# Two edits in a two-layer diffusion backbone: the low parts of the last tokens' normed activations from GpSimd to VectorE, and the first projection's matmuls between halves of the modulation's

## The chip, the cores and the metric

The kernel runs on one core of a Trainium2 chip. A core has TensorE (matrix multiplies into PSUM banks), VectorE, ScalarE and GpSimd (elementwise work), SyncE (here it only issues DMAs), an on-chip memory of 128 partitions (SBUF), and DMA queues to HBM. Each engine takes its own instructions strictly in order; engines wait for each other through semaphores. In the profile the engines are called PE (with PEld for its weight loads), DVE, ACT, POOL and SP. The metric is the device time of the whole program in microseconds, lower is better.

## The reference

Two trunk layers are computed for 512 latent tokens and 128 context tokens (640 tokens, five tiles of 128) with shared weights. What bears on this change is the shape of a layer: the activations are normed, scaled and shifted by a modulation that is itself a matrix product, and go into a wide projection; four mixers and a gated sum follow; then a second norm and a gated feed-forward network.

```
def trunk_layer(x, cond, lp, ctx):
    mod = jnp.matmul(jax.nn.silu(cond), lp['w_mod']) + lp['b_mod']
    sh1, sc1, ga1, sh2, sc2, ga2 = jnp.split(mod[:, None, :], 6, axis=-1)
    h = rmsnorm(x, lp['g_pre1']) * (1 + sc1) + sh1
    proj = jnp.matmul(h, lp['w_in'])
...
    mix = jnp.matmul(jnp.sum(gates * br, axis=2), lp['w_o'])
    x = x + ga1 * rmsnorm(mix, lp['g_post1'])
    h2 = rmsnorm(x, lp['g_pre2']) * (1 + sc2) + sh2
    gt, up = jnp.split(jnp.matmul(h2, lp['w_up']), 2, axis=-1)
    f = jnp.matmul(jax.nn.silu(gt) * up, lp['w_down'])
    x = x + ga2 * rmsnorm(f, lp['g_post2'])
```

## The kernel before, in words

All large products are made in float32 precision from two-part operands: a value is split into a high part that TensorE takes (a copy, made on ScalarE) and a low part, the value minus its high part (a subtraction, made on VectorE or GpSimd). A product is then three matmuls: high weight by high activation, high by low, low by high. Weight chunks are split in `wchunk` (ScalarE at L149, VectorE at L150).

Scheduling: the kernel is written in an order of work, but a scheduler that weighs planned durations sets the final order of instructions on each engine; the helper `after` pins one instruction behind another on an engine without any wait in hardware. Buffers rotate by tag (three for the high parts of weights, `whi`), so an instruction that fills a buffer waits until its last reader is done.

The first projection (`proj_tm`, layer 0). The modulation's weights arrive in 16 pieces of 256 KB pairs; each of its four quarters c is 64 small matmuls on 128 columns (L417), 16 for each of four pieces. After a quarter come an addition (L429), one transpose on TensorE (the `tr` of the code), the scale and shift of two of the eight 128-feature slices, and the high parts (L441, tile `hhi`) and low parts (L443, `hlo`) of those slices. The projection's own matmuls of the quarter before (`part(c - 1, ...)`, six matmuls of 496 columns for each of five token tiles) are placed behind the next quarter's modulation, with the transpose behind the first tile.

The passages between stages. At the end of `out_proj` the five token tiles i = 0 to 4 are finished one after the other (`post`, then `prenorm`): norm, eight transposes, eight scale-and-shift instructions shared by VectorE (L371) and ScalarE (L369), and the split in `norm_blocks`. That split makes, for each tile and each half q of the features, a high part on ScalarE (L1280) and a low part (L1282): on GpSimd for q = 0, on VectorE for q = 1. Tiles 3 and 4 belong wholly to the second token half; their q = 0 parts lie in two tiles called `U`, read by `ffn_first`, the first feed-forward matmuls on the second token half (four groups of 24 matmuls of 320 columns, tiles `psg`, `pss`). `combine` (L1293 and L1297) makes further sums of the same activations for the rest of the feed-forward network. Then follows the first product with the down weights, whose low part is made by L150. The passage from layer 0's feed-forward network to layer 1's projection uses the same code with the split inside `prenorm` (L375 high, L377 low, GpSimd for q = 0).

Of the kernel before, what the change touches and what calls it, by code (L numbers as in the profile page):

```python
# [21 lines left out]
NT = 5  # L22
# [84 lines left out]
class Step:  # L107
# [242 lines left out]
    def prenorm(self, i, x, M, which, hh):  # L350
        nc = self.nc
        s = 0 if i < 4 else 1
        xn = self.t("P", [128, SLOT])[:, :1024]
        ss = self.t("ss", [128, 1], bufs=4)
        r = self.t("rr", [128, 1], bufs=4)
        nc.scalar.activation(xn, x, AF.Square, accum_out=ss)
        self.rsqrt(r, ss, 1.0 / D)
        nc.scalar.activation(xn, x, AF.Copy, scale=r)
        tps = [self.ps("t"), self.ps("c")]
        h32 = xn.rearrange("p (k t) -> p k t", k=KT)  # L360
        for k in range(KT):
            self.tr(tps[k // 4][:, (k % 4) * 128:(k % 4) * 128 + 128], h32[:, k, :])
        sl = slice(i * 128, i * 128 + 128)
        for q in range(2):
            for k in range(4 * q, 4 * q + 4):
                a, b = M["A"][:, which, s, k:k + 1], M["B"][:, which, s, k:k + 1]
                tp = tps[q][:, (k % 4) * 128:(k % 4) * 128 + 128]
                if k % 2:
                    nc.scalar.activation(h32[:, k, :], tp, AF.Identity, bias=b, scale=a)  # L369
                else:  # L370
                    nc.vector.tensor_scalar(h32[:, k, :], tp, a, b, op0=ALU.mult, op1=ALU.add)  # L371
            ks = slice(4 * q, 4 * q + 4)
            if which:
                continue
            nc.scalar.activation(hh[0][:, ks, sl], h32[:, ks], AF.Copy)  # L375
            eng = nc.gpsimd if q == 0 else nc.vector
            eng.tensor_tensor(hh[1][:, ks, sl], h32[:, ks], hh[0][:, ks, sl], op=ALU.subtract)  # L377
        if which:
            self.norm_blocks(i, h32, hh)
            return h32  # L380
# [117 lines left out]
    def proj_tm(self, l, hh, norm):  # L498

        tmx = self.t("X", [128, 2 * SLOT])  # L500
        hs = (lambda k: hh[0][:, k, :], lambda k: hh[1][:, k, :])
        ps = [self.ps(t) for t in "gggss"]
        chs = {}

        def part(c, tiles):
            if c not in chs:
                chs[c] = self.tm_chunk(l, c)
            for i in tiles:
                ab = self.tmm(ps[i][:, :496], chs[c], (0, 1), hs, (2 * c, 2 * c + 1), i, c == 0, c == 3)
                if prev:  # L510
                    self.after(ab[0], prev[-1])
                    prev.append(ab[1])

        prev = []
        if norm:
            for c in range(4):
                mods = next(norm)
                if prev:
                    self.after(mods[0], prev[-1])
                chs[c] = self.tm_chunk(l, c)  # L520
                tr = next(norm)
                if c:
                    prev.append(mods[-1])
                    part(c - 1, range(1))
                self.after(tr, prev[-1] if prev else mods[-1])
                prev.append(tr)
                if c:
                    part(c - 1, range(1, NT))
            part(3, range(NT))
        else:  # L530
            for c in range(2):
                part(c, range(3))
                if self.late:
                    self.late.pop(0)()
            for c in range(2):
                part(c, range(3, NT))
            for c in range(2, 4):
                part(c, range(NT))
        out = []
        for i in range(NT):  # L540
            t = tmx[:, i * 496:i * 496 + 496]
            self.nc.scalar.copy(t, ps[i][:, :496])
            out.append(t)
        ab = tmx[:, :NT * 496].rearrange("p (i c) -> p i c", c=496)[:, :, 480:496]
        return out, ab
# [724 lines left out]
    def norm_blocks(self, i, h32, hb):  # L1270
        nc = self.nc
        for a, b in ((i * 128, min(i * 128 + 128, TH)), (max(i * 128, TH), i * 128 + 128)):
            if a >= b:
                continue
            second = a >= TH
            src, dst = slice(a - i * 128, b - i * 128), slice(a - TH * second, b - TH * second)
            for q in range(2):
                hi, lo = hb[3 * q if second else 1 + q]
                v = h32[:, 4 * q:4 * q + 4, src]
                nc.scalar.activation(hi[:, :, dst], v, AF.Copy)  # L1280
                eng = nc.gpsimd if q == 0 else nc.vector
                eng.tensor_tensor(lo[:, :, dst], v, hi[:, :, dst], op=ALU.subtract)  # L1282

    def combine(self, i, h32, hb):
# [324 lines left out]
```

## Time and profile before

| what | value |
|---|---|
| median of three runs | 2394.74 us (2394.31 to 2396.17) |
| the profiled execution, its own time | 2396.94 us |
| its span | 2395.1 us |
| mean granted TensorE clock in it | 0.989 of full speed |
| PE busy | 2291.1 us, 96% of the span |
| DVE busy | 1577.0 us, 66% |
| ACT busy | 984.2 us, 41% |
| POOL busy | 280.5 us, 12% |

TensorE is busy for nearly the whole span, so the 104 us in which it isn't (2395.1 less 2291.1), and the stretches at a lowered clock, are where a change of order can gain or lose. The clock has two levels here: 1.00 in a row is 2.4 GHz, 0.50 is 1.2 GHz.

### The profile page before, as it was taken

The numbers are of one execution on the slowest core, as the hardware profiler recorded it, in microseconds if no ns is written. First come the engines' busy times: TensorE is split into PE (matmuls) and PEld (weight loads), VectorE is DVE, ScalarE is ACT, GpSimd is POOL, SyncE is SP. The second block draws the span as 40 slices with busy tenths as digits, with TensorE's granted clock in tenths as the row PEclk, the third lists the DMA queues.
The fourth block names the chain that finished last, engine by engine and source line by source line (L and its number), as shares of the span: only waits on it lengthen the run. The fifth ranks groups of instructions, "written<-read, shape, count | busy, mean of one in ns | idle before, by whom it ended". The sixth has DMA issues, their size and how long they took to land. (4 is left out here: it accounts for less than half of the span.)

```text
span 2395.1 us, 38984 instructions
## 1 busy us (share of the span) xinstructions
PE 2291.1 (96%) x15094; PEld 2020.9 (84%) x15094; DVE 1577.0 (66%) x3370; ACT 984.2 (41%) x2046; POOL 280.5 (12%) x326
## 2 busy tenths in 40 slices
PE   7999999999999899999989999999999979999998
PEld 5877678989887889998878776889798869999997
DVE  5562787567357898666766538884763577667667
ACT  3351444233226534433564424532322355334433
POOL 0100113223022100000020002031310320000001
PEclk9999999999999999999999999999999989999999
DMA  8637213414434344222452561334253432223223
GB/s 263 168 118 214 68 58 99 126 51 111 134 127 140 98 134 141 78 71 93 121 154 73 157 205 30 99 85 100 60 137 124 129 123 71 88 72 106 71 89 114
DMA packets 328330, 269.48 MB, mean 113 GB/s; under 512 B 71552, under 2 KB 287232, under 8 KB 328144
## 3 DMA queue, kind: packets, MB, share of 16 engines
q1 hardware_dynamic: 328144, 266.98, 37.4%
q8 instruction: 119, 1.95, 0.3%
q14 instruction: 67, 0.55, 0.1%
HBM read 234.73 MB, written 32.20 MB: 111 GB/s over the span
## 5 line engine op out<-in xcount | busy, mean ns | idle before, releaser
L134 PE MATMUL psg<-hhi,whi 128*128 128x384 f32 (+2 forms) x1648 | 515.9, 320 | 11.7 <-DVE tg L1175 5.6
L134 PE MATMUL psg<-hhi,wlo 128*128 128x384 f32 (+2 forms) x1648 | 512.7, 318 | 2.2 <-DVE wlo L150 2.0
L134 PE MATMUL psg<-hlo,whi 128*128 128x256 f32 (+2 forms) x1568 | 504.0, 321 | 0.1
L150 DVE TENSOR_TENSOR wlo<-raw,whi 128x1024 fp32r<-128x1024 f32 (+1 forms) x176 | 219.5, 1248 | 208.2 <-ACT whi L149 205.5
L134 PEld LDWEIGHTS psg<-hhi,whi 128*128 128x128 f32 x1648 | 310.7, 190 | 22.9 <-DVE tg L1175 7.1
L134 PEld LDWEIGHTS psg<-hhi,wlo 128*128 128x128 f32 x1648 | 310.8, 190 | 15.5 <-issue 9.3
L134 PEld LDWEIGHTS psg<-hlo,whi 128*128 128x128 f32 x1568 | 298.2, 190 | 15.6 <-issue 13.2
L149 ACT ACTIVATE whi<-raw 128x1024 fp32r<-128x1024 f32 (+1 forms) x176 | 185.7, 1057 | 225.1 <-PE psg L134 166.6
L1144 ACT ACTIVATE tg<-psg 128x384 f32<-128x384 f32 (+1 forms) x128 | 54.9, 431 | 222.0 <-PE psg L134 203.1
L1337 ACT ACTIVATE wlo<-raw 128x512 fp32r<-128x512 f32 x120 | 75.8, 632 | 158.2 <-PE psc L134 91.4
L1323 DVE TENSOR_TENSOR wlo<-raw,wlo 128x512 fp32r<-128x512 f32 x120 | 82.8, 690 | 64.8 <-ACT wlo L1337 64.2
L134 PE MATMUL pss<-hhi,whi 128*128 128x320 f32 x504 | 122.9, 309 | 0.0
L134 PE MATMUL pss<-hhi,wlo 128*128 128x320 f32 x504 | 122.7, 308 | 0.0
L134 PE MATMUL psg<-oh,whi 128*128 128x384 f32 (+1 forms) x512 | 117.7, 315 | 3.8 <-DVE tg L1175 3.5
L134 PE MATMUL psg<-whi,U 128*128 128x512 f32 x356 | 118.7, 393 | 1.8 <-DVE U L157 1.3
L1177 POOL TENSOR_TENSOR acc<-acc,tg 128x640 f32<-128x640 f32 x48 | 85.3, 1780 | 241.8 <-DVE tg L1175 241.8
L1488 POOL TENSOR_TENSOR acc<-acc,oh 128x512 f32<-128x512 f32 x8 | 11.3, 1409 | 814.4 <-ACT dt L1487 808.4
L1323 DVE TENSOR_TENSOR whi<-raw,whi 128x512 fp32r<-128x512 f32 x120 | 82.3, 689 | 33.9 <-ACT whi L1337 33.9
L134 PE MATMUL pss<-whi,U 128*128 128x512 f32 x304 | 102.4, 391 | 0.8 <-DVE cv L1323 0.8
L134 PEld LDWEIGHTS psg<-oh,whi 128*128 128x128 f32 x512 | 85.0, 188 | 14.2 <-DVE tg L1175 6.9
L1337 ACT ACTIVATE whi<-raw 128x512 fp32r<-128x512 f32 x120 | 75.4, 631 | 41.5 <-DVE raw L1323 27.4
L134 PEld LDWEIGHTS pss<-hhi,whi 128*128 128x128 f32 x504 | 87.3, 188 | 0.0
(578 smaller groups left out, 5114.6 us busy)
## 6 DMA issues: line engine op xcount, KB each, us to landing
raw<-in_w_up SPq DMA_DIRECT2D x88, 512.0 KB, 3.6
raw<-in_w_in SPq DMA_DIRECT2D x86, 512.0 KB, 3.8
V<-in_w_mod SPq DMA_DIRECT2D x64, 512.0 KB, 4.7
raw<-in_w_down SPq DMA_DIRECT2D x44, 512.0 KB, 3.7
raw<-in_w_o SPq DMA_DIRECT2D x16, 512.0 KB, 3.8
V<-in_w_mod SPq DMA_DIRECT2D x32, 256.0 KB, 2.7
xs<-V SPq DMA_DIRECT2D x15, 512.0 KB, 3.4
V<-xs SPq DMA_DIRECT2D x15, 512.0 KB, 3.5
```

What stands on the lines that cost most here:

```text
L134: return self.nc.tensor.matmul(out, lhsT, rhs, start=start, stop=stop, skip_group_check=True)
L149: nc.scalar.activation(hi, raw[:, :a * b], AF.Copy)
L150: nc.vector.tensor_tensor(lo, raw[:, :a * b], hi, op=ALU.subtract)
L1144: self.nc.scalar.activation(tg[:, o:o + sz], p, AF.Tanh, scale=0.5)
L1177: nc.gpsimd.tensor_tensor(a, a, tg, op=ALU.add)
L1323: tt = lambda o, x, y, op: nc.vector.tensor_tensor(o, x, y, op=op)
L1337: nc.scalar.activation(hi, src, AF.Copy)
L1488: nc.gpsimd.tensor_tensor(y, y, G[0 if i < 4 else 1][:, 0:512], op=ALU.mult)
```

## The change

Two things change. In `prenorm` and `norm_blocks` the low parts of the feature half q = 0 stay on GpSimd for the token tiles 0 to 2 only; for tiles 3 and 4 VectorE makes them. In layer 0's `proj_tm`, quarters 1 to 3, the modulation's 64 small matmuls are cut into halves of 32: the first token tile of the projection's quarter before comes between the halves, the second tile behind the second half, and the transpose behind the second tile.

```diff
--- before.py
+++ after.py
@@ -373,7 +373,7 @@
             nc.scalar.activation(hh[0][:, ks, sl], h32[:, ks], AF.Copy)
-            eng = nc.gpsimd if q == 0 else nc.vector
+            eng = nc.gpsimd if q == 0 and i < 3 else nc.vector
             eng.tensor_tensor(hh[1][:, ks, sl], h32[:, ks], hh[0][:, ks, sl], op=ALU.subtract)
@@ -515,17 +515,21 @@
         if norm:
             for c in range(4):
                 mods = next(norm)
+                n = len(mods) // 2
                 if prev:
                     self.after(mods[0], prev[-1])
                 chs[c] = self.tm_chunk(l, c)
                 tr = next(norm)
                 if c:
+                    prev.append(mods[n - 1])
+                    part(c - 1, range(1))
+                    self.after(mods[n], prev[-1])
                     prev.append(mods[-1])
-                    part(c - 1, range(1))
+                    part(c - 1, range(1, 2))
                 self.after(tr, prev[-1] if prev else mods[-1])
                 prev.append(tr)
                 if c:
-                    part(c - 1, range(1, NT))
+                    part(c - 1, range(2, NT))
             part(3, range(NT))
@@ -1278,7 +1282,7 @@
                 nc.scalar.activation(hi[:, :, dst], v, AF.Copy)
-                eng = nc.gpsimd if q == 0 else nc.vector
+                eng = nc.gpsimd if q == 0 and i < 3 else nc.vector
                 eng.tensor_tensor(lo[:, :, dst], v, hi[:, :, dst], op=ALU.subtract)
```

GpSimd loses six instructions in all: two in each layer's passage inside the layer, two in the passage between the layers. Lines below the edit in `proj_tm` move down by four (L1282 becomes L1286).

On TensorE, at the second quarter of the modulation in the first projection, the rows before are these (`psc_315` is the modulation's bank, `psg_238` and `psg_239` the projection's first two token tiles, `cst` the identity of the transpose):

```order
L417 MATMUL psc_315<-T_327,cs_218 32x128 x8
L417 MATMUL psc_315<-U_338,cs_218 32x128 x8
L417 MATMUL psc_315<-acc_349,cs_218 32x128 x8
L134 MATMUL psg_238<-whi_296,hhi_74 128x496
...
L134 MATMUL psg_238<-whi_296,hlo_75 128x496
L139 MATMUL pst_368<-cst_63,oh_243 128x128
L134 MATMUL psg_239<-whi_296,hhi_74 128x496
```

and of the change, at the same place:

```order
L417 MATMUL psc_315<-T_327,cs_218 32x128 x8
L134 MATMUL psg_238<-whi_296,hhi_74 128x496
...
L134 MATMUL psg_238<-whi_296,hlo_75 128x496
L417 MATMUL psc_315<-U_338,cs_218 32x128 x8
L417 MATMUL psc_315<-acc_349,cs_218 32x128 x8
L134 MATMUL psg_239<-whi_296,hhi_74 128x496
...
L134 MATMUL psg_239<-whi_296,hlo_75 128x496
L139 MATMUL pst_368<-cst_63,oh_243 128x128
```

The first token tile has moved ahead of the modulation's last two pieces, and the transpose behind the second token tile. Quarters 3 and 4 read alike.

On VectorE, in layer 0's passage to the feed-forward network, the rows before are these (`P_7685` and `P_7752` are the scaled tiles 3 and 4, `U_7105` and `U_7106` the high and low parts of their q = 0 half):

```order
L371 TENSOR_SCALAR P_7752<-pst_7766,modA_235,modB_236 128x128
L371 TENSOR_SCALAR P_7752<-psc_7767,modA_235,modB_236 128x128
L1282 TENSOR_TENSOR hlo_7104<-P_7685,hhi_7103 128x4x128
L371 TENSOR_SCALAR P_7752<-pst_7766,modA_235,modB_236 128x128
L371 TENSOR_SCALAR P_7752<-psc_7767,modA_235,modB_236 128x128
L1293 TENSOR_TENSOR X_7851<-P_7889,X_7851 128x4x64
L1293 TENSOR_TENSOR T_7853<-P_7889,T_7852 128x4x64
L1293 TENSOR_TENSOR P_7929<-P_7929,hlo_7104 128x512
L1293 TENSOR_TENSOR P_7976<-P_7752,hhi_7103 128x512
L1282 TENSOR_TENSOR hlo_7104<-P_7752,hhi_7103 128x4x128
```

and of the change:

```order
L371 TENSOR_SCALAR P_7752<-pst_7766,modA_235,modB_236 128x128
L1286 TENSOR_TENSOR U_7106<-P_7685,U_7105 128x4x128
L1286 TENSOR_TENSOR hlo_7104<-P_7685,hhi_7103 128x4x128
L371 TENSOR_SCALAR P_7752<-pst_7766,modA_235,modB_236 128x128
L371 TENSOR_SCALAR P_7752<-psc_7767,modA_235,modB_236 128x128
L1297 TENSOR_TENSOR X_7851<-P_7889,X_7851 128x4x64
L1297 TENSOR_TENSOR T_7853<-P_7889,T_7852 128x4x64
L371 TENSOR_SCALAR P_7752<-psc_7767,modA_235,modB_236 128x128
L1297 TENSOR_TENSOR P_7929<-P_7929,hlo_7104 128x512
L1286 TENSOR_TENSOR U_7106<-P_7752,U_7105 128x4x128
L1286 TENSOR_TENSOR hlo_7104<-P_7752,hhi_7103 128x4x128
```

Two subtractions into `U_7106` have come in; the second stands ahead of the q = 1 subtraction of the same tile and behind one instruction of `combine`.

On ScalarE, a little later in the same passage, the rows before are these (`whi_8035` is the high part of the first down weights, `psg_7864` the bank of the first of `ffn_first`'s four groups):

```order
L1297 ACTIVATE X_7850<-P_7929 128x4x128
L1297 ACTIVATE hhi_7103<-P_7976 128x4x128
L149 ACTIVATE whi_8035<-raw_8033 128x1024
L1297 ACTIVATE X_7851<-P_7929 128x4x128
L1421 ACTIVATE tg_7944<-psg_7864 128x320
```

and of the change:

```order
L1301 ACTIVATE X_7850<-P_7929 128x4x128
L1301 ACTIVATE X_7851<-P_7929 128x4x128
L1425 ACTIVATE tg_7944<-psg_7864 128x320
L149 ACTIVATE whi_8035<-raw_8033 128x1024
L1301 ACTIVATE hhi_7103<-P_7976 128x4x128
```

The split of the down weights now stands ahead of the high part of tile 4's first sum instead of behind it.

## Rows read from the trace of the kernel before

**Rows 1.** The page's part 1: busy time of each engine.

```profile
PE 2291.1 (96%) x15094; PEld 2020.9 (84%) x15094; DVE 1577.0 (66%) x3370; ACT 984.2 (41%) x2046; POOL 280.5 (12%) x326
```

**Rows 2.** PE's waits over the span: for whom, total us, times, longest.

```profile
PE psg L134 <- POOL U L1282: 11.8, 2, 6.1
PE psg L134 <- POOL hlo L377: 1.0, 1, 1.0
```

**Rows 3.** Timeline of layer 0's passage: start us, duration us, engine, line.

```profile
777.44 1.28 POOL L1282 TENSOR_TENSOR U<-P,U 128x512 fp32r<-128x512 f32 x1 [15.11 <-ACT U L1280]
778.00 1.26 DVE L1282 TENSOR_TENSOR hlo<-P,hhi 128x512 fp32r<-128x512 f32 x1
...
780.33 0.62 ACT L1280 ACTIVATE U<-P 128x512 fp32r<-128x512 f32 x1
780.50 0.68 DVE L1293 TENSOR_TENSOR P<-P,hlo 128x512 f32<-128x512 f32 x1
...
781.00 0.52 PE L134 MATMUL psg<-U,whi 128*128 128x320 f32 x1 [2.48 <-ACT U L1280]
781.03 6.69 POOL L1282 TENSOR_TENSOR U<-P,U 128x512 fp32r<-128x512 f32 x1 [2.31 <-ACT U L1280]
...
785.91 0.68 DVE L1293 TENSOR_TENSOR P<-hhi,P 128x512 f32<-128x512 f32 x1
787.77 0.64 PE L134 MATMUL psg<-U,whi 128*128 128x320 f32 x1 [5.71 <-POOL U L1282]
```

**Rows 4.** Timeline of layer 1's passage, POOL and PE.

```profile
1963.91 6.69 POOL L1282 TENSOR_TENSOR U<-P,U 128x512 fp32r<-128x512 f32 x1 [2.31 <-ACT U L1280]
1970.65 0.63 PE L134 MATMUL psg<-U,whi 128*128 128x320 f32 x1 [6.05 <-POOL U L1282]
```

**Rows 5.** Busy by stretch: PE, PEld, DVE, ACT, POOL, then clock, DMA, GB/s.

```profile
26.80:37.05 10.25, 8.90 (x57) 6.22 (x58) 4.33 (x10) 2.87 (x5) 0.00 (x0) 0.50 1.04 347
37.05:65.70 28.65, 28.65 (x239) 23.48 (x238) 11.97 (x26) 10.30 (x19) 2.91 (x9) 1.00 0.76 206
...
781.16:791.40 10.24, 4.53 (x16) 4.13 (x17) 5.43 (x10) 2.06 (x4) 6.55 (x1) 0.50 0.00 0
...
1965.60:1975.80 10.20, 5.15 (x19) 5.15 (x20) 3.88 (x7) 1.23 (x2) 5.00 (x1) 0.50 0.00 0
```

**Rows 6.** Timelines behind layer 0's passage, ACT, DVE and PE.

```profile
792.93 1.06 ACT L149 ACTIVATE whi<-raw 128x1024 fp32r<-128x1024 f32 x1 [8.08 <-PE psg L134]
...
794.54 0.69 DVE L1293 TENSOR_TENSOR X<-P,X 128x512 fp32r<-128x512 f32 x1 [7.95 <-ACT X L1297]
...
801.06 1.22 DVE L150 TENSOR_TENSOR wlo<-raw,whi 128x1024 fp32r<-128x1024 f32 x1
...
803.13 0.40 PE L134 MATMUL pss<-whi,U 128*128 128x512 f32 x1
803.36 0.39 PE L134 MATMUL pss<-wlo,U 128*128 128x512 f32 x1
```

**Rows 7.** Timelines of the passage between the layers, POOL and PE.

```profile
1234.60 1.28 POOL L377 TENSOR_TENSOR hlo<-P,hhi 128x512 fp32r<-128x512 f32 x1 [6.15 <-ACT hhi L375]
...
1235.93 0.49 PE L134 MATMUL pss<-whi,hlo 128*128 128x496 f32 x1 [0.19 <-POOL hlo L377]
...
1239.53 0.50 PE L134 MATMUL pss<-whi,hlo 128*128 128x496 f32 x1 [0.19 <-POOL hlo L377]
```

**Rows 8.** Timelines of the first projection, DVE and PE.

```profile
28.00 0.82 DVE L443 TENSOR_TENSOR hlo<-X,hhi 128x640 fp32r<-128x640 f32 x1
...
28.32 1.75 PE L417 MATMUL psc<-U,cs 128*32 128x128 f32 x16
...
30.89 1.07 PE L417 MATMUL psc<-acc,cs 128*32 128x128 f32 x12 [0.49 <-DMA acc<-in_w_mod]
31.89 0.78 PE L134 MATMUL psg<-whi,hhi 128*128 128x496 f32 x1
...
34.12 0.61 PE L134 MATMUL psg<-whi,hlo 128*128 128x496 f32 x1
```

## The prediction

> **What bounds the kernel now.** I read the page's busy times first: PE is busy for 96% of the span, VectorE for 66%, GpSimd for 12% [rows 1]. TensorE sets the time nearly everywhere, so an edit on the other engines is worth only what PE waits for. The next view is therefore the waits of PE. For GpSimd's low parts in tile `U` (L1282) it waits 11.8 us in two waits, the longest 6.1, and for L377's 1.0 us in one [rows 2]; smaller ones come below.
>
> The third view is the timeline around the first of the two long waits. It shows why GpSimd is late. For tile 4 the high part on ACT runs 780.33 to 780.95, and GpSimd starts the low part at 781.03. The same instruction took GpSimd 1.28 us for tile 3 at 777.44; here it takes 6.69. PE does three matmuls from 781.00 and then waits 5.71 us, until 787.77 [rows 3]. Meanwhile VectorE runs ten two-operand instructions on 128x512 float32, one after another, the first at 780.50 and the last at 785.91 [rows 3]: one per 0.60 us ((785.91 less 780.50) over 9), 0.68 us each. GpSimd is done 1.1 us after the last of them ends (781.03 plus 6.69 against 785.91 plus 0.68). At tile 3 both engines work on such an instruction at once too, and there VectorE's takes 1.26 instead of 0.68 [rows 3]. So the two slow each other, and under a dense run of VectorE's GpSimd hardly advances. Layer 1 repeats it: GpSimd 6.69 us again, PE waits 6.05 [rows 4].
>
> The fourth view is the granted clock by stretch. It is 0.50 (1.2 GHz) in three stretches that concern this change: 26.80 to 37.05 in the first projection, 781.16 to 791.40 and 1965.60 to 1975.80 in the passages [rows 5].
>
> **The change, part by part.**
>
> *The passages inside the layers.* GpSimd loses both `U` subtractions, VectorE gains them. On VectorE each costs one slot of 0.60 us [rows 3]. The one for tile 4 stands behind one instruction of `combine`, so it starts when that ends or when the high part lands: 780.95 and, with GpSimd's gap from ACT's end, 781.03, plus up to 0.1 if the instruction ahead is still running. With 0.68 us it is done at 781.8, before PE has finished its three matmuls at 782.06 (787.77 less 5.71). The whole wait goes: 5.71 in layer 0 and 6.05 in layer 1 [rows 3, 4].
>
> A little more comes from the clock. PE restarts at 787.77 and the clock rises at 791.40, 3.63 us later; in layer 1 it restarts at 1970.65 and the clock rises at 1975.80, 5.15 later; in the projection PE is busy without a gap from 31.89 and the clock rises at 37.05, again 5.15 later [rows 3 to 5, 8]. Without the long wait PE works on from 781.0, and I take as the cold work that remains the smallest of these, 3.63 us, against 4.53 and 5.15 us of PE's cold busy time now [rows 5]. Work at half the clock takes twice as long, so half the difference is saved: 0.45 and 0.75 us. Bounds: if 5.15 us stay cold, nothing or a loss of 0.3; if the clock doesn't fall at all, half of 4.53 and 5.15, that is 2.3 and 2.6.
>
> What is late next? The first `ffn_first` group ends 6 us sooner, and with it the high part of the down weights (`whi`, at 792.93, released by PE) and VectorE's run from 794.54, which had stood 7.95 us for ACT queued behind it. The low part `wlo` runs 801.06 to 802.28, and PE takes it at 803.36 [rows 6]: a margin of 1.1 us. Of VectorE's two added slots (1.2 us), 0.6 is given back, since its q = 1 subtraction for tile 3 no longer runs against GpSimd (1.26 to 0.68). In the new order of ScalarE the split of the down weights also stands one instruction earlier. So I expect a margin of about 0.5 us left, and price this at nothing; the cover is the 7.95 us in which VectorE had stood idle. If it is gone, the two slots and a matching delay for the next chunks cost 1 to 3 us per layer (rival 1).
>
> A rule that speaks against the move: the Trainium skill, "SBUF — State Buffer", section "SBUF: two separate sides", says that VectorE and GpSimd take a shared port pair by an exclusive lock, held by whoever starts first for the whole instruction. By it alone GpSimd would have been blocked for one VectorE instruction, not ten; it would have finished near 783, and the change would be worth about 1 us for each passage and the time about 2390. The row shows 6.69 us under ten instructions, so the lock is here at best taken again and again by VectorE, and I go by the row.
>
> Sum of both passages: 5.71 + 6.05 + 0.45 + 0.75 = 13.0 us.
>
> *The passage between the layers.* GpSimd's L377 takes 1.28 us at 1234.60 and PE waits 0.19 us for it at 1235.93 and once more 0.19 at 1239.53 [rows 7]. On VectorE a 0.68 us instruction replaces it: 0.4 us gained. Bounds 0 (VectorE late by as much) to 1.4 (with the single wait of 1.0 in rows 2, if that too belongs here).
>
> *The first projection.* PE's time from 28.32 to 31.89 goes to the second half of the modulation's quarter, with a wait of 0.49 us for a DMA at 30.89; then come the projection's matmuls [rows 8]. Their last operand, `hlo` of the second slice, is ready at 28.00 plus 0.82, so the first token tile could stand there from 28.82. Put there, it covers the DMA wait (0.5 us), and PE runs without a gap from about 28.8. Then the clock should rise 3.63 to 5.15 us later, at 32.4 to 34.0 instead of 37.05; of those 3.1 to 4.6 us half is gained, 1.5 to 2.3. Against this stand, in three quarters, one more switch each between the two kinds of matmul. Now such a switch shows no gap: twelve small matmuls from 30.89 take 1.07 us, and the first wide one starts at 31.89 [rows 8]. I price it at 0.1 us, at most 0.2. The transpose comes behind one more tile, and I see nothing that waits for it, with the next quarter's matmuls long behind: nothing, and in the low end of the range. Together: from 0.5 - 0.6, about 0 (clock as before), to 0.5 + 2.3, 2.8. I take 0.5 + 1.5 - 0.3 = 1.7 us, with the later of the two rises.
>
> **The sum.** 13.0 + 0.4 + 1.7 = 15.1 us. The profiled execution took 2396.94 us and would take 2381.8; it lay 2.2 us above the median, which gives 2379.6, **2380 us** in round numbers. All terms at their ends: 11.8 - 0.3 + 0 - 0.1 = 11.4 us at the low end, 11.8 + 4.9 + 1.4 + 2.8 = 20.9 at the high one, or 2383 to 2374.
>
> **The rivals.**
>
> *1. VectorE becomes the bound behind the passages.* Its margin on `wlo` was 1.1 us and two slots are 1.2 [rows 3, 6]. For it: the gain moves PE's need 6 us forward, VectorE's work only as far as its idle time allows. Against: that idle time, 7.95 us, is larger than the gain. 1 to 3 us lost per passage: 2382 to 2386, faster still. The Trainium skill, "Perfetto Trace Analysis", section "Optimizing Scalar/DVE Operations", advises taking work off a saturated VectorE, the reverse of this move; VectorE is busy for 66% of the span, so by the trace that applies only to the stretch behind the passage.
>
> *2. The clock doesn't fall in the passages.* In layer 1 it fell at 1965.60, 1.0 us into the wait that goes (1970.65 less 6.05 is 1964.60), which speaks for it; in layer 0 it fell at 781.16, after the 2.48 us wait for ACT that stays [rows 3 to 5], which speaks against. It gives 3.7 us more (2.3 + 2.6 less 1.2): 2376. In layer 1 alone, 1.9 more: 2378.
>
> *3. The change doesn't do what it says.* VectorE takes the new subtraction only behind its ten instructions, as a wait of an earlier one in its queue holds it. Then it ends near 787.8 (785.91 + 0.68 + 1.2), as late as GpSimd; only the 2.1 us of the other two parts remain, 2392.6. Against: in the new order only one instruction of `combine` stands ahead of it.
>
> *4. Slower.* The modulation's pieces between the token tiles (they are short matmuls of 128 columns with DMA waits) keep the projection at 1.2 GHz. At most that costs as much again as the hot stretch of 28.65 us [rows 5], 2394.7 + 28.65 less 13.4 (13.0 and 0.4), or 2410. It decides from 13.4 us of that stretch run cold on. Against: that stretch holds the later quarters' modulation with its short matmuls already, and the clock stayed at 1.00 throughout.
>
> **How the numbers follow.** My forecast 0.68, rival 1 0.12, rival 2 0.12, rival 3 0.05, rival 4 0.03. What a measurement of this kernel can tell from no change is about 0.2%, 4.8 us. Faster by more than that: all but the last two, 0.92; within: 0.05; slower: 0.03. The range takes in rivals 1 and 2, as it must to reach 8 in 10 with the unknown costs: 2375.5 to 2386.
>
> **What would show it.** Right: no wait of PE for GpSimd's `U`; VectorE's `U` subtraction done some 0.8 us after ACT's high part; `ffn_first` ends 6 us sooner; the cold stretches of the passages shorter; the first projection's clock up before 35. Wrong: a wait of PE for VectorE's `wlo` or `U` in the passage; a cold stretch as long as before; PE waits for DMA in the projection's third or fourth quarter that were hidden. Much above 2386 means that the wait moved to another engine.

## The result, and the profile after

| what | before | after |
|---|---|---|
| median of six runs | 2395.45 us (2392.47 to 2402.15) | 2383.32 us (2378.68 to 2386.68) |
| the profiled execution | 2396.94 us | 2385.14 us |
| its span | 2395.1 us | 2383.4 us |

The ratio is 0.9944, with an interval of 0.9927 to 0.9961: 13.4 us off 2395.45, or 9.3 to 17.5. The forecast was 2380 us, 2375.5 to 2386.

The first view is again PE's waits over the span: for whom, total us, times, longest. These rows of after answer to [rows 2]:

```profile
PE psg L134 <- ACT U L1284: 4.3, 2, 2.1
...
PE psg L134 <- POOL hlo L377: 1.0, 1, 1.0
...
PE psg L134 <- DVE U L1286: 0.5, 1, 0.5
```

This row of before belongs beside the first of them:

```profile
PE psg L134 <- ACT U L1280: 5.0, 2, 2.5
```

The 11.8 us for GpSimd's `U` are gone. What replaces them is 0.5 us for VectorE's; the waits for ScalarE's high part are 0.7 us shorter. The 1.0 us for L377 has stayed, so it belongs to a tile that GpSimd kept; the two waits of 0.19 us [rows 7] are gone.

The timeline of layer 0's passage in after (start, duration, engine), which answers to [rows 3] and [rows 6]:

```profile
784.78 0.62 ACT L1284 ACTIVATE U<-P 128x512 fp32r<-128x512 f32 x1
785.26 0.68 DVE L1297 TENSOR_TENSOR P<-P,hlo 128x512 f32<-128x512 f32 x1
785.45 0.41 PE L134 MATMUL psg<-U,whi 128*128 128x320 f32 x1 [2.14 <-ACT U L1284]
785.86 0.69 DVE L1286 TENSOR_TENSOR U<-P,U 128x512 fp32r<-128x512 f32 x1
786.70 0.38 PE L134 MATMUL psg<-U,whi 128*128 128x320 f32 x1 [0.54 <-DVE U L1286]
...
798.96 1.22 DVE L150 TENSOR_TENSOR wlo<-raw,whi 128x1024 fp32r<-128x1024 f32 x1
...
800.62 0.39 PE L134 MATMUL pss<-wlo,U 128*128 128x512 f32 x1
```

From PE's first matmul on `U` to the one that needs its low part it is now 1.25 us (785.45 to 786.70), and it was 6.77 [rows 3]. VectorE's subtraction starts only behind the one instruction of `combine` ahead of it, at 785.86, or 0.46 us after ScalarE's high part landed (784.78 plus 0.62), so PE waits 0.54 us. The down weights' low part ends at 800.18 and is needed at 800.62: a margin of 0.44 us is left of 1.1.

Busy time by stretch in after (PE, PEld, DVE, ACT, POOL, clock, DMA share, GB/s):

```profile
776.00:806.00 30.00, 26.86 (x169) 24.86 (x168) 29.59 (x64) 20.46 (x40) 0.00 (x0) 1.00 0.21 63
1955.00:1990.00 35.00, 32.63 (x179) 29.57 (x179) 28.02 (x48) 21.96 (x42) 0.00 (x0) 0.95 0.16 46
...
545.00:562.50 17.50, 17.50 (x66) 13.56 (x66) 10.17 (x22) 4.08 (x9) 5.64 (x6) 0.61 0.17 45
```

In layer 0's passage the clock didn't fall at all, where it had been 0.50 for 10.24 us [rows 5]; in layer 1's it is 0.95 over 35 us, which is some 3.4 us at 0.50. VectorE is busy for 29.59 of 30 us. The last row is a surprise far from any edit: the clock was 0.61 over 17.5 us, 13.65 us of it at 0.50.

To see where the time went, I compared the starts of the same PE instruction in two kernels. This table (my own working from PE's timelines) says by how much each stage grew (+) or shrank (-) in us against the profile of before: the stages end at the matmuls that start at 66.14, 760.71 to 804.50, and 1933.81 to 1994.07 us in before. "Rest" is the change of the whole span less these three. In brackets stands for how many us the clock was at 0.50 in that stage of that kernel; such a stretch is called a spell below. The names are those of the experiments below.

```
kernel          first projection   passage 0      passage 1      rest           span
before               (10.2)            (13.6)         (13.7)         (10.3)
after           -0.3 (10.2)       -8.0  (0.0)    -8.2  (3.4)    +4.7 (17.1)   -11.7
e4_again        -3.0  (3.4)       -5.6  (6.8)    -5.9 (10.2)    +5.0 (20.5)    -9.5
e10_after       -3.9  (3.4)       -7.0  (3.4)    -7.0  (6.8)    +0.5 (17.1)   -17.3
e1_passages     +0.6 (10.2)       -7.0  (3.4)    -6.0 (10.2)    +0.9  (6.8)   -11.4
e3_tile4        -2.2  (6.8)       -4.8  (9.5)    -9.1  (0.0)    +1.8 (11.0)   -14.3
e2_projection   -3.1  (3.4)       +0.7 (10.2)    -0.4 (13.7)    +2.7  (6.8)    -0.2
e9_hold         -1.5 (10.2)       -4.0 (10.2)    -4.5 (10.2)    +3.2 (13.7)    -6.7
```

The passages carry the gain in every kernel that has their edit. How much each carries goes with the spells: in passage 0 it is 8.0 us without one, 7.0 with 3.4 us, 5.6 with 6.8 and 4.8 with 9.5, and passage 1 reads alike. The rest moves by up to 5 us, in one and the same program too (after, e4_again, e10_after). The two largest values belong to profiles with a spell of 13.65 us in the rest, but e10_after, with 17.1 us at 0.50 as in after, has only +0.5: the spells explain a part of this scatter, and the other part stays open.

### The profile page after: what moved, and what is told of

Read it like the earlier page. It is cut to its first block, busy times and chain, and to the rows that moved or that the text cites. A ratio compares the mean times of both kernels' runs of the same rounds, so it can differ in the third digit from the quotient of the medians.

```text
span 2383.4 us, 38978 instructions
## 1 busy us (share of the span) xinstructions
PE 2289.3 (96%) x15094; PEld 2016.6 (85%) x15094; DVE 1578.9 (66%) x3376; ACT 983.5 (41%) x2046; POOL 262.0 (11%) x320
## 5 line engine op out<-in xcount | busy, mean ns | idle before, releaser
L1327 DVE TENSOR_TENSOR whi<-raw,whi 128x512 fp32r<-128x512 f32 x120 | 82.4, 689 | 33.8 <-ACT whi L1341 33.8
L1341 ACT ACTIVATE whi<-raw 128x512 fp32r<-128x512 f32 x120 | 75.4, 630 | 43.7 <-DVE raw L1327 29.6
```

The costliest lines, as they stand in the source:

```text
L1327: tt = lambda o, x, y, op: nc.vector.tensor_tensor(o, x, y, op=op)
L1341: nc.scalar.activation(hi, src, AF.Copy)
```

## The experiments

**The edits one at a time, and the change again.** Four kernels on one chip. *e1_passages* has only the edits of `prenorm` and `norm_blocks`:

```diff
-eng = nc.gpsimd if q == 0 else nc.vector
+eng = nc.gpsimd if q == 0 and i < 3 else nc.vector
```

> Only the two edits that move low parts from GpSimd to VectorE; the first projection as before. Theory A (the time came from PE's waits for GpSimd in the two passages, with the clock that the passages got back): about 13 us off, 2382 us, ratio 0.9944 or so, no wait of PE for GpSimd's U, and in each passage no more than one cold spell. Theory B (a good part of the 12 us came from the projection edit or from clock spells elsewhere): less than 10 us off, above 2386 us.

Measured: 2382.58 us, 0.9943 (0.9928 to 0.9958). The two passages alone give as much as the whole change; Theory B falls. The "no more than one cold spell" didn't hold in layer 1, where the profile has two (1937.2 to 1944.1 and 1961.1 to 1964.5 us).

*e2_projection* has only the edit of `proj_tm`.

> Only the projection edit; both GpSimd edits left out. Theory A, as predicted: 1.7 us off, 2393.7 us, ratio 0.9993; the clock rises near 34 instead of 37, and the stage after the projection starts 1.5 to 2 us sooner. Rival (the pieces' DMAs set the projection's pace, so PE only waits elsewhere): within 0.5 us of before, PE's DMA waits in the first 60 us as long in sum as before. Both: PE still waits 11.8 us for GpSimd's U.

Measured: 2396.94 us against 2396.73, 1.0000 (0.9986 to 1.0015). The interval holds both the predicted 1.7 us (0.9993) and nothing. Its waits of PE show that nothing else was touched:

```profile
PE psg L134 <- POOL U L1286: 12.1, 2, 6.1
```

The stage itself is easier to read than the time. Busy time by stretch, before:

```profile
26.40:38.00 11.60, 10.21 (x67) 7.13 (x66) 5.53 (x12) 3.77 (x7) 0.00 (x0) 0.56 1.04 349
```

e2_projection:

```profile
26.40:38.00 11.60, 11.58 (x111) 8.62 (x115) 7.22 (x14) 4.26 (x7) 0.00 (x0) 0.86 0.98 329
```

and after:

```profile
26.40:38.00 11.60, 9.60 (x82) 6.92 (x83) 4.99 (x10) 3.51 (x7) 0.00 (x0) 0.71 1.06 353
```

The clock over these 11.6 us is higher with the edit, but it also varies without it (0.71 in e1_passages). Counted from the start to the mixer's first matmul (66.14 us in before) it is clearer: at 0.50 for 10.2 us in each of the four profiles without the edit, for 3.4 us in four, 6.8 in three and 10.2 in one of the eight with it. In e2_projection the clock rose for the last time in that stage at 29.6 us, not near 34 as expected. The rival is half right: PE's waits for the pieces' DMAs come to 5.2 us there and to 4.8 in before, so they have not become less. Over eight profiles with the edit (after and the kernels e2, e3, e4, e7, e8, e10, e11) the mixer's first matmul came 0.3 to 3.9 us sooner than in before, 2.5 in the mean; over four without it (before and e1, e6, e9) from 1.5 sooner to 0.6 later, 0.6 sooner in the mean. The difference of the means is 2.0 us, and the two groups overlap.

*e3_tile4* leaves tile 3 to GpSimd inside the layers (`i < 4` in `norm_blocks`).

> The changed kernel, but inside the layers GpSimd keeps tile 3's low part of q = 0, and only tile 4's goes to VectorE. Theory A (only tile 4's subtraction was late): all of the gain stays, 2383 us; VectorE has one 0.60 us slot less ahead of tile 4's last scale-and-shift, so ACT's high part of tile 4 comes up to 0.6 us sooner and PE waits 1.5 to 2.1 us for it instead of 2.1: up to 1.2 us faster. Rival (GpSimd is slow wherever VectorE works): tile 3's takes several us and PE waits for it, 2386 us or more.

Measured: 2383.51 us, 0.9946 (0.9932 to 0.9961), the same as the change. GpSimd's subtraction for tile 3 and PE's waits in layer 0's passage:

```profile
774.58 1.29 POOL L1286 TENSOR_TENSOR U<-P,U 128x512 fp32r<-128x512 f32 x1 [16.30 <-ACT U L1284]
```

```profile
778.16 0.42 PE L134 MATMUL psg<-U,whi 128*128 128x320 f32 x1 [2.50 <-ACT U L1284]
...
779.08 0.39 PE L134 MATMUL psg<-U,whi 128*128 128x320 f32 x1 [0.21 <-DVE U L1286]
```

Tile 3's low part was never the trouble: only tile 4's had to move. The hope of a sooner high part failed: PE waits 2.50 us for ACT, not less than 2.14.

*e4_again* is the changed kernel, unaltered.

> The changed kernel once more, unaltered, for its profile. In its first profile the clock was low for 13.65 us between 545 and 560 us, with the same waits of PE there as before within 1 us, and 3.4 us at 15 to 22. If these are chance, they are missing here or lie elsewhere, and the profiled run is 4 to 7 us shorter; if the change brings them about, they are there again. Time 2383 us, ratio 0.993 to 0.996.

Measured: 2381.93 us, 0.9941 (0.9922 to 0.9961). The spell at 545 us isn't there, in this profile or in e10_after's; e4_again:

```profile
545.00:562.50 17.50, 17.50 (x110) 16.18 (x110) 10.36 (x19) 4.82 (x7) 5.17 (x4) 1.00 0.57 136
```

So the program doesn't bring it about in each execution at that place. It came again in e8_more (544.6 to 558.3 us). In e4_again a spell of the same length lies elsewhere, again with PE busy throughout:

```profile
1717.10:1730.70 13.60, 13.60 (x44) 10.00 (x43) 6.15 (x14) 3.96 (x9) 4.04 (x4) 0.50 0.07 12
```

The profiled run was therefore not 4 to 7 us shorter than the first but 2.3 us longer (2387.43 against 2385.14). What sets these spells off stays open.

**The disputed cost by itself.** *e5_alone* puts a probe ahead of the kernel: GpSimd's 128x512 subtraction beside VectorE runs of several kinds.

```diff
...
+for kind, one in (("none", 0), ("two", 0), ("five", 0), ("psum", 0), ("one", 0), ("two", 1), ("one", 1), ("none", 0)):
+    n, f = run[kind]
+    last = sub(C[:, h], A[:, h], G[:, h])
+    if one:
+        g = nc.gpsimd.tensor_scalar(G[:, h], C[:, h], 2.0, 1.0, op0=ALU.mult, op1=ALU.add)
+    else:
+        g = nc.gpsimd.tensor_tensor(G[:, h], A[:, h], C[:, h], op=ALU.subtract)
+    for j in range(n):
+        x = f(j)
...
```

> The changed kernel with a probe put ahead of its work (nothing is left out; some 60 us are added, so its time is not compared). The probe runs GpSimd's subtraction on 128x512 float32 eight times, one after the other, beside VectorE runs of different kinds: none; ten two-operand subtractions; five; ten with one operand from PSUM; ten with a single operand; then GpSimd with a single operand beside ten two-operand and ten one-operand ones; none again. Theory A (VectorE's two-operand instructions hold GpSimd up for as long as they come back to back): 1.3 us alone, 6.2 to 7 beside ten, 3 to 4 beside five, and about 1.3 to 2 beside ten with a single operand. Rival (the lock of the Trainium skill's page on SBUF, taken for one instruction at a time and then free for the other): at most 2 us in every case. Second rival (6.69 us came from the operands or the place in the program): 1.3 us in every case.

Measured, GpSimd's eight instructions in the order of that list:

```profile
6.41 1.26 POOL L260 TENSOR_TENSOR acc<-P,P 128x512 f32<-128x512 f32 x1 [4.57 <-DVE P L245]
9.85 1.64 POOL L260 TENSOR_TENSOR acc<-P,P 128x512 f32<-128x512 f32 x1 [2.18 <-DVE P L245]
17.54 4.05 POOL L260 TENSOR_TENSOR acc<-P,P 128x512 f32<-128x512 f32 x1 [6.04 <-DVE P L245]
22.39 1.27 POOL L260 TENSOR_TENSOR acc<-P,P 128x512 f32<-128x512 f32 x1 [0.81 <-DVE P L245]
28.97 1.37 POOL L260 TENSOR_TENSOR acc<-P,P 128x512 f32<-128x512 f32 x1 [5.32 <-DVE P L245]
34.01 6.41 POOL L258 TENSOR_SCALAR acc<-P 128x512 f32<-128x512 f32 x1 [3.66 <-DVE P L245]
41.23 0.73 POOL L258 TENSOR_SCALAR acc<-P 128x512 f32<-128x512 f32 x1 [0.81 <-DVE P L245]
45.59 1.27 POOL L260 TENSOR_TENSOR acc<-P,P 128x512 f32<-128x512 f32 x1 [3.64 <-DVE P L245]
```

and VectorE's runs beside the second to the seventh:

```profile
9.69 7.17 DVE L245 TENSOR_TENSOR P<-P,P 128x512 f32<-128x512 f32 x10
...
17.38 3.09 DVE L245 TENSOR_TENSOR P<-P,P 128x512 f32<-128x512 f32 x5
...
22.23 6.07 DVE L245 TENSOR_TENSOR P<-pst,P 128x512 f32<-128x512 f32 x10
...
28.81 4.51 DVE L252 TENSOR_SCALAR P<-P 128x512 f32<-128x512 f32 x10
...
33.84 6.10 DVE L245 TENSOR_TENSOR P<-P,P 128x512 f32<-128x512 f32 x10
...
41.06 3.85 DVE L252 TENSOR_SCALAR P<-P 128x512 f32<-128x512 f32 x10
```

With no run beside it 1.26 (VectorE does only 128x1 work and one copy then). Beside five two-operand instructions 4.05: GpSimd ends 1.12 us after the run does (17.54 + 4.05 less 17.38 + 3.09), as it did in before (1.13). Both rivals fall with that: they had at most 2 us, and 1.3 us, in every case. Even its one-operand instruction takes 6.41 beside ten two-operand ones and 0.73 beside one-operand ones. With an operand in PSUM the same run holds nothing up (1.27). The miss is the second row: beside ten, GpSimd took only 1.64, and VectorE paid (7.17 instead of 6.10; its second instruction alone took 1.75). So one of the two wins, and GpSimd can: Theory A in its strict form ("6.2 to 7 beside ten") holds in one of the two cases. What decides stays open; both started 0.16 us behind VectorE's first.

**GpSimd given its turn.** *e9_hold* leaves all work where it was in the kernel before and only makes VectorE stand still:

```diff
-eng.tensor_tensor(lo[:, :, dst], v, hi[:, :, dst], op=ALU.subtract)
+self.hold(i, q, eng.tensor_tensor(lo[:, :, dst], v, hi[:, :, dst], op=ALU.subtract))
...
+def _hold(self, i, q, ins):
+    if i == 4 and q == 0:
+        self.held = ins
+    elif i == 4:
+        self.follow(ins, self.held)
...
```

> The kernel before with one wait added and the order of every engine unchanged: in the passages inside the layers VectorE's q = 1 subtraction of tile 4 waits until GpSimd's q = 0 subtraction of that tile is done. GpSimd keeps all its work. Theory A (GpSimd gets nothing done while VectorE runs two-operand instructions back to back): GpSimd starts at some 781, gets its turn when VectorE stands at the wait 0.7 to 0.8 us later, and takes 1.9 to 2.2 us instead of 6.69; PE restarts some 4.6 us sooner in each layer and the clock gives back some of it: 9 to 11 us off, 2385 to 2387 us if before is 2396. Rival (GpSimd itself is slow on these operands, so that VectorE was the faster engine for them): GpSimd takes 6 us or more, VectorE's work behind the wait is late, and nothing is gained or time is lost.

Measured: 2390.05 us against 2396.76, 0.9970 (0.9953 to 0.9987). GpSimd in layer 0's passage:

```profile
781.57 1.88 POOL L1282 TENSOR_TENSOR U<-P,U 128x512 fp32r<-128x512 f32 x1 [2.31 <-ACT U L1280]
```

VectorE's q = 1 subtraction:

```profile
783.48 0.69 DVE L1282 TENSOR_TENSOR hlo<-P,hhi 128x512 fp32r<-128x512 f32 x1 [1.16 <-POOL U L1282]
```

and PE:

```profile
783.50 0.64 PE L134 MATMUL psg<-U,whi 128*128 128x320 f32 x1 [1.07 <-POOL U L1282]
```

The same engine on the same operands takes 1.88 instead of 6.69 us, only because VectorE pauses for 1.16. The pause begins at 782.32 (783.48 less 1.16), and GpSimd is done 1.13 us later (781.57 plus 1.88), the same 1.1 us as behind the end of a run. PE's wait falls from 5.71 to 1.07, in layer 1 from 6.05 to 1.25. This shows the cause. The time won, 6.7 us (3 to 11), is less than the 9 to 11 that I expected, though the interval reaches into it: in that profile the two stages shrank by 8.4 us, with 10.2 us still at 0.50 in each, and the rest of the span grew by 3.2.

**The clock's share.** *e6_fill* adds 40 matmuls into PE's wait in the kernel before.

```diff
...
+for j in range(n):
+    d = self.mm(p, w[0][:, j % KT, :], x[:, j % 4, :])
+    self.after(d, prev)
...
```

> The kernel before with 40 matmuls of 128x320 added on PE in each passage (their result is not used), ahead of the one that waits for GpSimd's low part; they take 5.9 us at full clock and lie inside the wait. It shows what of the gain is clock and what is wait. By my sum the clock part is 1.2 us in both passages (3.6 us of each stay cold after the 2.5 us wait for ACT): 2394 us. If the long wait kept the clock down alone (rival 2 of the prediction), the cold stretches of 10.2 us fall to 0 or 3.4 and up to 4.9 us come off: 2390.5 us. GpSimd's subtraction takes 6.7 us as before, since VectorE's work is the same.

Measured: 2409.40 us, 1.0037 (1.0023 to 1.0050), slower by 0.4%. The time says nothing on the clock, since the scheduler moved more of `combine` into VectorE's run. The run's last two-operand instruction on SBUF:

```profile
790.12 0.68 DVE L1293 TENSOR_TENSOR P<-hhi,P 128x512 f32<-128x512 f32 x1
```

GpSimd beside it, and PE behind the 40 matmuls:

```profile
780.42 11.51 POOL L1282 TENSOR_TENSOR U<-P,U 128x512 fp32r<-128x512 f32 x1 [2.31 <-ACT U L1280]
```

```profile
780.65 7.58 PE L134 MATMUL pst<-hhi,whi 128*128 128x320 f32 x40
791.98 0.63 PE L134 MATMUL psg<-U,whi 128*128 128x320 f32 x1 [3.76 <-POOL U L1282]
```

My expectation of 6.7 us for GpSimd failed, and the failure tests the mechanism: from GpSimd's start the run goes on for 10.4 us (to 790.80) instead of 5.6 (781.03 to 786.59), and GpSimd's instruction is longer by the same 4.8 us; in both kernels it ends 1.13 us behind the run. What ends the run here is an instruction with an operand in PSUM (L1423, at 790.73).

The profile does say something on the clock. Busy time by stretch, e6_fill:

```profile
781.32:784.74 3.42, 3.42 (x15) 3.42 (x14) 3.42 (x7) 1.79 (x4) 3.42 (x1) 0.50 0.00 0
784.74:791.56 6.82, 3.49 (x24) 3.22 (x22) 6.82 (x13) 1.95 (x4) 6.82 (x1) 1.00 0.00 0
791.56:794.98 3.42, 3.00 (x11) 3.00 (x12) 0.92 (x1) 0.00 (x0) 0.37 (x1) 0.50 0.02 5
```

With PE at work on the 40 matmuls instead of waiting, the spell behind the wait for ScalarE's `U` lasts 3.42 us and not 10.24; the clock falls once more behind the new wait of 3.76 us. So the long wait is what had kept the clock down, and a short spell belongs to the wait that stays.

The passages of the other runs agree. Behind PE's wait for ACT's `U`, where before had 10.24 and 10.20 us at 0.50, the kernels that moved tile 4's subtraction had no such spell or one of 3.4 us. Spells of 3.4 to 6.8 us at an earlier wait, some 20 us ahead, come and go from profile to profile, in before too.

**Going on.** *e7_ahead* makes tile 4's scale-and-shift on VectorE sooner (`PRI_N` is 150).

```diff
-nc.vector.tensor_scalar(h32[:, k, :], tp, a, b, op0=ALU.mult, op1=ALU.add)
+self.ahead(which and i == 4, lambda: nc.vector.tensor_scalar(h32[:, k, :], tp, a, b, op0=ALU.mult, op1=ALU.add))
...
+with self.tc.high_priority(PRI_N):
+    return f()
...
```

> The changed kernel with VectorE's four scale-and-shift instructions of tile 4 put ahead in the passages inside the layers (in front of tile 3's q = 1 low part and of combine's X and T). What PE now waits for there is ACT's high part of tile 4, 2.1 us in each layer, and in layer 0 then 0.5 us for VectorE's low part. Theory: these instructions are what ACT waits for, so PE restarts some 0.9 us sooner in each layer: 2 us in all, 0.9985 of the changed kernel, which only the profile can tell. Rival: the low part then comes last and PE waits as long for it instead: no gain.

Measured: 2378.35 us, 0.9908 (0.9889 to 0.9928). Its waits of PE:

```profile
PE psg L134 <- ACT U L1284: 3.9, 2, 1.9
...
PE psg L134 <- DVE U L1286: 0.4, 2, 0.2
```

That is 0.5 us less than in after, so the time was more than its cause. *e8_more* keeps that and adds tile 2 between the layers (`i < 2` in `prenorm`).

> As the last one, and in the passage between the layers tile 2's low part of q = 0 goes to VectorE too: PE waits 1.0 us for GpSimd there in the changed kernel. Theory: that 1.0 us goes, another 1 us in all: 2380 us. Rival: VectorE's new place for it is as late, and the 1.0 us stays under VectorE's name.

Measured: 2382.73 us, 0.9924 (0.9904 to 0.9944); the wait for GpSimd is gone, and in its place PE waits 0.4 us for VectorE's `hlo`. Gained 0.6 us at that place, below what the time can tell. To settle e7_ahead it ran once more, with the changed kernel on the same chip.

> The changed kernel unaltered, on the same chip as the next run, as its partner. 0.994 of before, and a fourth look at where its low-clock spells lie.

> The changed kernel with VectorE's scale-and-shift of tile 4 put ahead, once more, beside the changed kernel on one chip. Its first run gave 0.9908 of before, while the waits that it removed in its profile come to less than 1 us (PE's wait for ACT's high part 3.9 instead of 4.3 us in sum). If that is its worth, it is within 0.001 of its partner, 0.993 to 0.994; if the order is worth more through the clock, it stays 5 us or more below its partner.

Measured: 2381.86 us, 0.9942 (0.9925 to 0.9959), for the change; 2382.44 us, 0.9932 (0.9911 to 0.9953), for e11_ahead. The two can't be told apart: the first 0.9908, measured on a chip on which the changed kernel itself didn't run, isn't borne out. No version is shown to beat the change.

## Why the prediction was right

**The wait.** Predicted: both long waits go, 11.76 us. They went, with 0.54 us for VectorE in layer 0 as the price. That wait was one of my signs of being wrong, on a small scale, and two readings in its sum were off. I let at most 0.1 us of the instruction ahead be left when the high part lands, and it held VectorE for 0.46 us, so the subtraction is done 1.15 us after the high part and not 0.8; and PE does its three matmuls in 0.71 us at full clock, not 1.06, so it comes to the wait sooner. ACT's high part cost PE 0.34 us less (2.14 instead of 2.48). That GpSimd is held up by VectorE's run is shown in both directions: e9_hold interrupts the run and GpSimd takes 1.88 us, e6_fill makes it longer and GpSimd takes 11.51.

**The clock in the passages.** Predicted 1.2 us, from 3.63 us of cold work left in each, between nothing and 4.9. Measured: no cold spell behind that wait or one of 3.4 us. The stages shrank by 5.6 to 8.2 us, 13.6 for the two in the mean of the four profiles of after, e1, e4 and e10; predicted were 13.0. The waits account for 12.0 of them (11.8 + 5.0 in before, 4.3 + 0.5 in after), which leaves 1.6 us for the clock and all else. Rival 2 (the clock doesn't fall) came true in some passages, as in layer 0's in after, and not in others; what decides between the two these runs don't show.

**VectorE's margin** on `wlo`: predicted 0.5 us, measured 0.44. Rival 1 didn't happen, though VectorE is busy for 29.59 of 30 us there. The Trainium skill, "Perfetto Trace Analysis", section "Optimizing Scalar/DVE Operations", says that taking work off a saturated VectorE may make sense, and adds that between VectorE and GpSimd it might not help. Here the engine that was full in that stretch took work over, and apart from the 0.54 us PE had no wait for VectorE there; the trace decides.

**Between the layers.** The two waits of 0.19 us went, 0.4 as predicted; the 1.0 us stayed. Over a longer stretch the spells hide its worth. In the narrow one between PE's matmuls that start at 1228.50 and 1245.05 us in before, the four profiles without the edit take 16.54 or 16.55 us. With it, six of the eight take 15.8 to 16.4 and the two with a spell in it (e1 and e7) 17.3. So 0.2 to 0.7 us are gained there without a spell.

**The first projection** came out near its sum, but not by its terms. I had the token tile start at 28.8 us, when its last operand is ready. PE's timeline in after, beside [rows 8]:

```profile
29.40 1.07 PE L417 MATMUL psc<-T,cs 128*32 128x128 f32 x12 [1.93 <-DMA T<-in_w_mod]
30.40 0.78 PE L134 MATMUL psg<-whi,hhi 128*128 128x496 f32 x1
```

PE stands 1.93 us for the second piece, which lies in the half that stays in front, so the tile starts at 30.40 there; why the piece was so late isn't shown. That is this profile alone: in the other seven with the edit the tile starts at 27.7 to 29.2 us, as forecast, and in the four without it at 31.5 to 33.9. The term that failed is the 0.5 us of covered DMA wait: up to the mixer, PE's waits for the pieces come to 4.0 us in the mean of the eight profiles and to 4.1 of the four. The clock, in turn, rose sooner than the 34.0 that I took: for the last time in the stage at 28.9 to 34.1 us, below 33 in seven of the eight, and at 33.8 to 37.1 without the edit. So the stage's 2.0 us in the mean of profiles lie near the 1.7 in part by luck: one term was too high, the other too low. The whole time of e2_projection shows neither that gain nor its absence.

**The time.** 2383.3 against 2380: inside the range, 3.3 us above. Before lay 0.7 us higher in the six runs than in the three I had, so the gain was 12.1 us by medians and 13.4 by the ratio, where I had 15.1. The interval holds 15.1. Rival 3 is excluded by VectorE's wait of 0.5 us, rival 4 by the clock of the later projection, which stayed at 1.00.

**The rule that I set aside.** By the Trainium skill, "SBUF — State Buffer", section "SBUF: two separate sides", whoever starts first holds the pair for its whole instruction. The probe agrees in what takes part: a run with one operand in PSUM holds GpSimd up not at all (1.27 us), and one with both in SBUF does. It differs in how long: not one instruction of VectorE, but the whole back-to-back run, 4.05 us for five and 11.51 for the long one. By the rule the time would have been near 2390 us, by the row 2380; 2383.3 was measured, and the interval of the gain (9.3 to 17.5 us) leaves out the rule's 5 us.

## What to carry to other kernels

When an instruction on GpSimd takes several times what its twin takes, look at what VectorE runs beside it: a back-to-back run of two-operand SBUF instructions can hold it until 1.1 us after the run ends. Then a short low-latency instruction belongs on the engine that is busy, in front of the run, or the run needs a pause in the right place; the share of busy time says nothing on this. Where single profiles scatter by 5 us, in part through the clock, compare the length of the stage that the edit touches, over several profiles, before the whole time.

## What the runs showed of the hardware that was not expected

GpSimd can also win against a dense run: 1.64 us beside ten, with VectorE's run at 7.17 instead of 6.10 us. For tile 4 in the passages of before and of e6_fill it lost each time. For tile 3 in before it had started 0.56 us ahead, and there VectorE's instruction took 1.26 us [rows 3]. In the probe it won from a start 0.16 us behind and, with the same start, lost; what decides was not found.

A spell at clock 0.50 of 13.65 us came in the middle of a stretch where PE was busy for all of 17.5 us, in two of eight profiles of kernels with the projection edit, and cost about 6 us: between the matmuls at 545.44 and 560.16 us in after, which stand 14.72 us apart, against 547.37 and 556.10, 8.73 apart, in before. No edit is near it. A spell of that length also came at 1717.1 us in e4_again and, 36 us later by the probe's length, in e5_alone. None came in the four profiles without the projection edit; four of nine against none of four is too little to call the edit its cause or to clear it.
